# Six persistent places instead of four rotating ones for the split halves of the experts' weights, and two raw buffers fewer

## The chip, the core and the metric

One core of a Trainium2 chip runs the whole program. The metric is device time in microseconds (us), from start to end of one execution; the number given for a kernel is the median of several. Five engines of the core matter: PE (matrix multiplication), ACT (scalar engine), DVE (vector engine), POOL and SP. Here SP issues nearly all transfers.

## What is computed

The reference is a small network on 256 tokens of width 1024: a first block of four mixers with a feed-forward part, then a second block with a retention mixer, a dense feed-forward part, a Fourier mixer, and last a mixture of eight experts. All of it is float32. The experts are the part that the change is about:

```
def swiglu(t, w_gate, w_up, w_down):
    return (jax.nn.silu(t @ w_gate) * (t @ w_up)) @ w_down

def moe_swiglu(h, w_router, w_gate, w_up, w_down):
    ...
    top_val, top_idx = lax.top_k(logits, TOP_K)
    top_w = jax.nn.softmax(top_val, axis=-1)
    gates = jnp.sum(jax.nn.one_hot(top_idx, N_EXPERTS, dtype=jnp.float32) * top_w[..., None], axis=1)
    ...
    for e in range(N_EXPERTS):
        out = out + gates[:, e:e + 1] * swiglu(t, w_gate[e], w_up[e], w_down[e])
```

## The kernel before

All weights lie in memory as 475 units of 1 MB, a tile of 128 partitions by 2048 float32 each, in the order in which they are used. SP loads one unit after another into raw tiles. To multiply in float32 precision on PE, each weight is split into two parts that PE takes at full rate: ACT copies a half unit (128 by 1024) into `wh`, the rounded high part (line 128), and DVE subtracts it from the raw half into `wl`, the low part (line 129). So each of the 950 halves costs one ACT and one DVE instruction, and PE works on both parts. `split()` (line 117 on) writes these two instructions for the next half and appends the pair to the list `wq`; `half()` calls `split()` once and takes the oldest pair from the list, and with `ahead=False` it only takes. How far the splits run ahead of the matmuls in the written program is thus the length of `wq`. The tiles of `wh` and of `wl` rotate through a pool `wp` of four places each: the split of half n can't write before PE has read half n-4.

An expert runs 84 halves in seven strips. A strip s consists of
- a gate strip: four halves, six matmuls each (per half two blocks of `wh` with the high part of the tokens `ex`, `wh` with their low part, `wl` with their high part: lines 1142 to 1144). Between its second and third half stands `turn(s-1)`, eight small matmuls that transpose the previous strip's `h` (line 1194);
- `sg`, the Silu of the gate result on ACT (line 1177), which needs the last matmul of the gate strip;
- an up strip: four halves in two pairs;
- `h` on DVE (line 1184), the product of `sg` and the up result, which needs the last matmul of the up strip;
- `hx`, the split of the transposed previous `h` (ACT line 1200, DVE line 1201);
- `down(s-1)`: four halves in two pairs.

Pairs of halves in up and down stand in a branch that PE alone decides at run time (lines 1146 to 1153): an expert with at most 64 tokens takes the packed form, in which one matmul with line 1139 stands for the two of lines 1142 and 1143, so that PE has four matmuls per half instead of six. In the profiled execution experts 0, 2, 3 and 4 are packed, 1, 5, 6 and 7 are not. ACT and DVE do the same work in both.

Within an expert I count halves locally: strip s (from 1) has gate halves 8+12(s-1) to 11+12(s-1), then four of up, then four of down(s-1). Strip 3 thus has the gate halves 32 to 35, the up halves 36 to 39 and the down halves 40 to 43, and strip 4's gate halves begin at 44.

The order of PE and SP is the one in which the code is written. The order of ACT and DVE is set when the program is built, by a scheduler that places each instruction by a model of when its inputs are there; the engine then keeps that order. `turn`, `hx`, `sg` and `h` have a priority in it (`tc.high_priority`).

The raw tiles come from pools: `rawp` of 6 units, `raw2p` of 4, `raw3p` of 2, `raw4p` of 2 (opened just ahead of the experts), and the former tile of the tokens, `xT`, of 1: 15 in the experts. A raw tile is loaded anew as soon as both its halves are split.

Of the kernel before, what the change touches and what calls it, by code (L numbers as in the profile page):

```python
# [10 lines left out]
F32R = mybir.dt.float32r  # L11
# [5 lines left out]
P = 128  # L17
# [46 lines left out]
def kernel(  # L64
# [9 lines left out]
):  # L74
    nc = tc.nc
    NU = ws_d.shape[0]
    WB = 4
    HP = 300
    HQ = 512
    HU = UN // 2  # L80

    NRAW, R2N, R3N, R4N = 6, 4, 2, 2
    const = ctx.enter_context(tc.tile_pool(name="const", bufs=1))
    rawp = ctx.enter_context(tc.tile_pool(name="rawp", bufs=NRAW))
    wp = ctx.enter_context(tc.tile_pool(name="wp", bufs=WB))
    psp = ctx.enter_context(tc.tile_pool(name="psp", bufs=2, space=bass.MemoryType.PSUM))
    ctx.enter_context(tc.manual_schedule(engines={mybir.EngineType.PE, mybir.EngineType.SP}))

# [2 lines left out]
    wq = []  # L91
# [18 lines left out]
    def more_room(name, n):  # L110
        pool = ctx.enter_context(tc.tile_pool(name=name, bufs=n))
        for _ in range(n):
            fetch(pool)

    half_ = [0, 0]

    def split(scales=None, between=None):


        if not raw or (half_[1] == H_F2 and scales is None):  # L120
            return
        half_[1] += 1
        r = raw[0][0][:, half_[0] * HU:(half_[0] + 1) * HU]
        wh = wp.tile([P, HU], F32R, tag="wh", name="wh")
        wl = wp.tile([P, HU], F32R, tag="wl", name="wl")
        if scales is None:
            for o in (slice(0, HQ), slice(HQ, HU)) if half_[1] == 1 else (slice(0, HU),):
                nc.scalar.activation(out=wh[:, o], in_=r[:, o], func=AF.Copy)  # L128
                nc.vector.tensor_tensor(out=wl[:, o], in0=r[:, o], in1=wh[:, o].bitcast(F32), op=ALU.subtract)  # L129
                if between is not None and o.start == 0:  # L130
                    between()
        else:
            for t in range(2):
                o = slice(t * 512, t * 512 + 512)
                nc.scalar.activation(out=wh[:, o], in_=r[:, o], func=AF.Copy, scale=scales[:, t:t + 1])
                nc.vector.scalar_tensor_tensor(out=wl[:, o], in0=r[:, o], scalar=scales[:, t:t + 1],
                                               in1=wh[:, o].bitcast(F32), op0=ALU.mult, op1=ALU.subtract)
        wq.append((wh, wl))
        if half_[0]:
            fetch(raw.pop(0)[1])  # L140
        half_[0] ^= 1
# [8 lines left out]
    def advance(item):  # L150
        try:
            item[0] = next(item[1]) or 1
        except StopIteration:
            side.remove(item)
# [16 lines left out]
    def half(ahead=True):  # L171

        for item in list(side):
            item[0] -= 1
            if item[0] <= 0:
                advance(item)
        if ahead:
            split()
        return wq.pop(0)

    def bank(tag="mm", shape=(P, 2, S)):
        return psp.tile(list(shape), F32, tag=tag, name=tag, bufs={"mm": 4, "sd": 2, "dn": 2}[tag])
# [3 lines left out]
    def mm3T(ps, u, b, xh, xl, start, stop):  # L186
        wh, wl = u
        c = slice(b * P, (b + 1) * P)
        mm(ps, wh[:, c], xh, start=start, stop=False)  # L189
        mm(ps, wh[:, c], xl, start=False, stop=False)  # L190
        mm(ps, wl[:, c], xh, start=False, stop=stop)  # L191
# [10 lines left out]
    def unit_late(xh, xl, late=2):  # L202

        ps = [bank("mm", (P, S)) for _ in range(2)]
        us = []
        for cb in range(2):
            us.append(half())
            for k in range(KD - late):
                mm3T(ps[cb], us[cb], k, xh[:, k], xl[:, k], k == 0, False)
        for cb in range(2):  # L210
            for k in range(KD - late, KD):
                mm3T(ps[cb], us[cb], k, xh[:, k], xl[:, k], False, k == KD - 1)
        return ps

    def stripX(xh, xl, mid=None):
# [51 lines left out]
    def col(c, n=1):  # L267
        return cols[:, c:c + n]
# [94 lines left out]
    for c in range(2, KD, 2):  # L363
        resplit(c, 2, col(C_N1, 8))
    for _ in range(WB - 2):
        split()
# [692 lines left out]


    pt.close()
    if R4N:
        more_room("raw4p", R4N)
    xT_flat = xT.rearrange("p a b -> p (a b)")
    fetch(xT_flat)
    fn = xT_flat[:, 0:D]
    with ExitStack() as pe:
# [48 lines left out]
        def experts(ex, rs, half_fn, hooks=None, n_of=None):  # L1116
# [6 lines left out]
            n = [0]  # L1123
# [3 lines left out]
            def nexth(**kw):  # L1127
                if hooks and n[0] in hooks:
                    hooks[n[0]]()
                n[0] += 1  # L1130
                return half_fn(**kw)
# [76 lines left out]
            def down(s, mid=None):  # L1208
                def blocks(b0):
                    pair(lambda w, packed: hi_lo(ht[s], [down_item(s, b0 + i, w[i], hf) for i in range(2) for hf in range(2)],  # L1210
                                                 packed))

                blocks(0)
                if mid is not None:
                    mid()
                if s < 6:
                    blocks(2)
                else:

                    w = [nexth() for _ in range(2)]  # L1220
                    for hf in range(2):
                        either(lambda packed: hi_lo(ht[s], [down_item(s, b, w[b - 2], hf) for b in (2, 3)], packed))
                        with tc.high_priority(HP):
                            result(hf)

            res = []

            def result(hf):
                y = G2.tile([P, 2, 512], F32R, tag="hx", name="y")
                yh, yl = y[:, 0], y[:, 1]  # L1230
                nc.scalar.activation(out=yh, in_=pd[hf], func=AF.Copy)
                nc.vector.tensor_tensor(out=yl, in0=pd[hf], in1=yh.bitcast(F32), op=ALU.subtract)
                res.append((yh, yl))
# [30 lines left out]
        for i in (0, 2, 1, 3):  # L1264
            nxt[3][i]()
        finish_rms()
        last = None
        for e in range(E):
            ex, sot, rs, _ = nxt
# [34 lines left out]
        with tc.tile_pool(name="O", bufs=1) as O:  # L1304
            ecur = O.tile([P, E], F32, name="ecur")
            emask = O.tile([P, E], F32, name="emask")
            epos = O.tile([P, 2], F32, name="epos")
            egts = O.tile([P, 2], F32, name="egts")
            etmp = O.tile([P, 2, E], F32, name="etmp")
            with tc.If(n_over[0] + n_over[1] > 0):  # L1310

                nc.vector.tensor_copy(out=ecur, in_=io8)
                with tc.For_i(0, E, 1) as ev:
                    nc.vector.tensor_scalar(out=emask, in0=ecur, scalar1=-8.0, scalar2=None, op0=ALU.is_equal)
                    for src, dst in ((pos, epos), (gts, egts)):
                        nc.vector.tensor_tensor(out=etmp, in0=src, in1=emask.unsqueeze(1).to_broadcast([P, 2, E]), op=ALU.mult)
                        nc.vector.tensor_reduce(out=dst, in_=etmp, axis=AX.X, op=ALU.add)
                    nc.vector.tensor_scalar(out=epos, in0=epos, scalar1=float(-P), scalar2=None, op0=ALU.add)
                    cnt_ = [0]
                    cur_ = []  # L1320

                    def ohalf(ahead=True):
                        i, h = divmod(cnt_[0], 2)
                        if h == 0:
                            t = rawp.tile([P, UN], F32, tag="raw", name="oraw")
                            nc.sync.dma_start(t, ws_d[bass.ds(ev * UE + (NU - E * UE + i), 1)].rearrange("a p n -> p (a n)"))
                            cur_[:] = [t]
                        r = cur_[0][:, h * HU:(h + 1) * HU]
                        wh = wp.tile([P, HU], F32R, tag="wh", name="owh")
                        wl = wp.tile([P, HU], F32R, tag="wl", name="owl")  # L1330
                        nc.scalar.activation(out=wh, in_=r, func=AF.Copy)
                        nc.vector.tensor_tensor(out=wl, in0=r, in1=wh.bitcast(F32), op=ALU.subtract)
                        cnt_[0] += 1
                        return wh, wl

                    oex, osot, ors, steps = gather(lambda t: epos[:, t:t + 1], lambda t: epos[:, t:t + 1])
                    for f in steps:
                        f()
                    combine(experts(oex, ors, ohalf), osot, lambda t: egts[:, t:t + 1])
                    nc.vector.tensor_scalar(out=ecur, in0=ecur, scalar1=-1.0, scalar2=None, op0=ALU.add)  # L1340
                for hf in range(2):
                    out_sumsq(hf)
                out_rms()
# [172 lines left out]
```

## Time and profile before

| what | value |
|---|---|
| time, median of 3 runs | 1873.32 us (1871.12 to 1874.76) |
| time of the profiled execution | 1872.74 us |
| its span | 1871.0 us |
| PE busy | 1817.4 us, 97% of the span |
| DVE busy | 1482.0 us, 79% |
| ACT busy | 1210.6 us, 65% |
| POOL busy | 158.2 us, 8% |
| split of a half on DVE, line 129 | 906 instructions, 1227 ns each |
| split of a half on ACT, line 128 | 906 instructions, 1053 ns each |

The experts run from about 900 us to the end. The span is what the trace covers; the 1.7 us up to the time of the execution lie around it. In rows of the trace an instruction shows its start, its duration and, in brackets, the idle time of its engine ahead of it with what ended that. Consecutive instructions of an engine overlap a little, so that the step from start to start can be shorter than a duration.

### The profile page before, as it was taken

Reading aid. Unit: us, or ns where it says so; the run is one execution under the profiler, and the core shown is the slowest. Engines: PE = TensorE matmul, PEld = TensorE weight load, DVE = VectorE, ACT = ScalarE, POOL = GpSimd, SP = SyncE. Lnnn points to the kernel's source line nnn. Section 1 sums busy time; section 2 is a strip of 40 time slices with the busy share of each in tenths; the row PEclk is TensorE's granted clock in tenths of the full one; section 3 lists DMA queues with packets and bytes.
Section 4 is the critical chain, followed back from the end, with each engine's and each line's share of the span. In section 5 each row is a group of like instructions: output and inputs, shape, how many; then the busy total and the mean of one; then the engine's idle time right before and its main releaser. Section 6 shows DMA issues by size and latency. Waiting matters only on the chain. (4 is left out here: it accounts for less than half of the span.)

```text
span 1871.0 us, 28740 instructions
## 1 busy us (share of the span) xinstructions
PE 1817.4 (97%) x10890; PEld 1574.5 (84%) x10890; DVE 1482.0 (79%) x1855; ACT 1210.6 (65%) x1484; POOL 158.2 (8%) x154
## 2 busy tenths in 40 slices
PE   8999999999999999999999999999999999999997
PEld 7999999999888999998777887777777788888885
DVE  5666676657677666656899989999999998988987
ACT  5765454455344444446787777888878777777775
POOL 2302122211111122110000000000000000000000
PEclk9999999999999999999999999999999999999999
DMA  8344544555444564544799998999999999999970
GB/s 313 140 154 168 193 178 183 181 181 197 158 150 159 189 248 184 187 170 180 295 419 377 353 367 326 411 386 377 415 354 413 381 353 364 332 356 354 343 290 36
DMA packets 71156, 505.77 MB, mean 270 GB/s; under 512 B 7888, under 2 KB 8016, under 8 KB 10320
## 3 DMA queue, kind: packets, MB, share of 16 engines
q1 hardware_dynamic: 70992, 503.53, 70.7%
q8 instruction: 110, 1.80, 0.4%
q14 instruction: 54, 0.44, 0.1%
HBM read 502.45 MB, written 1.05 MB: 269 GB/s over the span
## 5 line engine op out<-in xcount | busy, mean ns | idle before, releaser
L129 DVE TENSOR_TENSOR wl<-raw,wh 128x1024 fp32r<-128x1024 f32 (+1 forms) x906 | 1078.5, 1227 | 235.3 <-ACT wh L128 226.2
L128 ACT ACTIVATE wh<-raw 128x1024 fp32r<-128x1024 f32 (+1 forms) x906 | 922.0, 1053 | 428.9 <-PE mm L190 188.7
L189 PE MATMUL mm<-xh,wh 128*128 128x256 f32 x1248 | 357.5, 286 | 6.7 <-ACT xh L342 6.7
L1144 PE MATMUL mm<-wl,ex 128*128 128x512 f32 x896 | 356.0, 397 | 3.7 <-DVE wl L129 3.7
L190 PE MATMUL mm<-xl,wh 128*128 128x256 f32 x1248 | 355.2, 285 | 1.0 <-DVE xl L343 0.7
L191 PE MATMUL mm<-xh,wl 128*128 128x256 f32 x1248 | 354.9, 284 | 0.8 <-DVE wl L129 0.8
L1142 PE MATMUL mm<-wh,ex 128*128 128x512 f32 x672 | 270.4, 402 | 0.0
L1143 PE MATMUL mm<-wh,ex 128*128 128x512 f32 x672 | 266.1, 396 | 0.2 <-DVE ex L1103 0.2
L189 PEld LDWEIGHTS mm<-xh,wh 128*128 128x128 f32 x1248 | 237.9, 191 | 8.2 <-ACT xh L342 6.7
L190 PEld LDWEIGHTS mm<-xl,wh 128*128 128x128 f32 x1248 | 237.9, 191 | 2.4 <-DVE xl L343 2.3
L191 PEld LDWEIGHTS mm<-xh,wl 128*128 128x128 f32 x1248 | 237.7, 190 | 1.1 <-DVE wl L129 1.0
L1144 PEld LDWEIGHTS mm<-wl,ex 128*128 128x128 f32 x896 | 168.6, 188 | 54.2 <-DVE wl L129 13.7
L1144 PE MATMUL dn<-wl,hx 128*128 128x512 f32 x448 | 183.6, 410 | 12.1 <-DVE wl L129 11.9
L1143 PEld LDWEIGHTS mm<-wh,ex 128*128 128x128 f32 x672 | 126.7, 189 | 28.2 <-DVE ex L1103 0.5
L1142 PEld LDWEIGHTS mm<-wh,ex 128*128 128x128 f32 x672 | 126.6, 188 | 26.0 <-ACT wh L128 0.3
L1144 PEld LDWEIGHTS dn<-wl,hx 128*128 128x128 f32 x448 | 84.2, 188 | 55.8 <-DVE wl L129 40.1
L190 PE MATMUL mm<-hl,wh 128*128 128x256 f32 x352 | 99.8, 283 | 0.0
L191 PE MATMUL mm<-hh,wl 128*128 128x256 f32 x352 | 99.8, 283 | 0.0
L189 PE MATMUL mm<-hh,wh 128*128 128x256 f32 x352 | 99.8, 283 | 0.0
L1139 PE MATMUL dn<-wh,hx 128*128 128x512 f32 x224 | 89.2, 398 | 0.0
L1142 PE MATMUL dn<-wh,hx 128*128 128x512 f32 x224 | 88.9, 397 | 0.0
L1139 PE MATMUL mm<-wh,ex 128*128 128x512 f32 x224 | 88.7, 396 | 0.0
(400 smaller groups left out, 2500.7 us busy)
## 6 DMA issues: line engine op xcount, KB each, us to landing
raw<-in_ws_dram SPq DMA_DIRECT2D x451, 1024.0 KB, 6.3
xT<-in_ws_dram SPq DMA_DIRECT2D x22, 1024.0 KB, 7.0
raw<-in_ws_dram SPq DMA_DIRECT2D x3, 512.0 KB, 6.3
xT<-in_xT_dram SPq DMA_DIRECT2D x4, 256.0 KB, 5.4
xT<-in_xT_dram SPq DMA_DIRECT2D x1, 1024.0 KB, 8.3
out_dram<-acc SPq DMA_DIRECT2D x4, 256.0 KB, 2.1
cstA<-in_cst_dram SPq DMA_DIRECT2D x1, 576.0 KB, 9.1
raw<-in_ws_dram SPq DMA_DIRECT2D x2, 256.0 KB, 4.5
```

The costliest lines, as they stand in the source:

```text
L128: nc.scalar.activation(out=wh[:, o], in_=r[:, o], func=AF.Copy)
L129: nc.vector.tensor_tensor(out=wl[:, o], in0=r[:, o], in1=wh[:, o].bitcast(F32), op=ALU.subtract)
L189: mm(ps, wh[:, c], xh, start=start, stop=False)
L190: mm(ps, wh[:, c], xl, start=False, stop=False)
L191: mm(ps, wl[:, c], xh, start=False, stop=stop)
L1139: mm(out_, e, wh, start=first, stop=False)
L1142: mm(out_, e, wh, start=first, stop=False)
L1143: mm(out_, xk[:, P:2 * P], wh, start=False, stop=False)
L1144: mm(out_, e, wl, start=False, stop=last)
```

## The change

In the code before, `wp.tile(...)` is asked for each half. Now two tiles of four places (`ringh`, `ringl`) are made once, and two tiles of two places (`extrah`, `extral`) just ahead of the experts, in the memory that `raw4p` had. The function `place(i)` says which place the i-th split writes: one of four until the extra tiles exist, then one of six in turn. The written program splits further ahead: two more halves before the first expert (the `while`), and `half(ahead=not cb)` and `nexth(ahead=False)` with a `split()` behind the pair where `half()` had split for each half of a pair. So five halves stand in `wq` where three stood.

```
-    WB = 4
+    WB, WX = 4, 2
...
-    NRAW, R2N, R3N, R4N = 6, 4, 2, 2
+    NRAW, R2N, R3N = 6, 4, 2
...
-    wp = ctx.enter_context(tc.tile_pool(name="wp", bufs=WB))
+    wp = ctx.enter_context(tc.tile_pool(name="wp", bufs=1))
+
+    ring = [wp.tile([P, WB, HU], F32R, name=f"ring{n}") for n in "hl"]
+    extra = []
+
+    def place(i):
+        if extra and i >= extra[0]:
+            j = (i - extra[0]) % (WB + WX)
+            if j < WX:
+                return [x[:, j] for x in extra[1]]
+            i = extra[0] + j - WX
+        return [x[:, i % WB] for x in ring]
...
+        wh, wl = place(half_[1])
         half_[1] += 1
         r = raw[0][0][:, half_[0] * HU:(half_[0] + 1) * HU]
-        wh = wp.tile([P, HU], F32R, tag="wh", name="wh")
-        wl = wp.tile([P, HU], F32R, tag="wl", name="wl")
...
-            us.append(half())
+            us.append(half(ahead=not cb))
...
+        split()
         return ps
...
-    if R4N:
-        more_room("raw4p", R4N)
+    wp3 = ctx.enter_context(tc.tile_pool(name="wp3", bufs=1))
+    extra[:] = [half_[1], [wp3.tile([P, WX, HU], F32R, name=f"extra{n}") for n in "hl"]]
...
-                    w = [nexth() for _ in range(2)]
+                    w = [nexth(), nexth(ahead=False)]
...
+                    if half_fn is half:
+                        split()
...
+        while len(wq) < WB + WX - 1:
+            split()
```

The raw buffers of the experts are 13 instead of 15. No engine gets an instruction more or less. What moves is the order on ACT and DVE. In the kernel after, line 128 is line 139, 129 is 140, 1177 is 1189, 1184 is 1196, 1200 is 1212 and 1201 is 1213.

First, ACT in strip 3 of expert 2 (packed). Before: the row of four is halves 33 to 36, the next row is 37, the two ahead of `sg` are 38 and 39, and half 40 stands behind it.

```order
684 L128 ACTIVATE wh<-raw 128x1024 x4
685 L1150 UNCONDITIONAL_BRANCH
686 L128 ACTIVATE wh<-raw 128x1024
687 L1200 ACTIVATE hx<-sd 128x4x128
688 L128 ACTIVATE wh<-raw 128x1024 x2
689 L1177 ACTIVATE sg<-mm,rsl 128x512
690 L1150 UNCONDITIONAL_BRANCH
691 L128 ACTIVATE wh<-raw 128x1024
```

After: rows 742 and 743 are halves 33 to 35, row 745 is 36 and 37, and row 748, behind `sg`, is 38.

```order
742 L139 ACTIVATE extrah<-raw 128x1024
743 L139 ACTIVATE ringh<-raw 128x1024 x2
744 L1162 UNCONDITIONAL_BRANCH
745 L139 ACTIVATE ringh<-raw 128x1024 x2
746 L1212 ACTIVATE hx<-sd 128x4x128
747 L1189 ACTIVATE sg<-mm,rsl 128x512
748 L139 ACTIVATE extrah<-raw 128x1024
749 L1162 UNCONDITIONAL_BRANCH
750 L139 ACTIVATE extrah<-raw 128x1024
```

`sg` of strip 3 stood behind half 39 and stands behind half 37. It is so in strips 2 to 6 of experts 2 to 7 and in strips 4 to 6 of expert 1. In expert 0 and in the strips of expert 1 ahead of these, the row reads the other way: there, halves 38, 39, 40 and 41 (or those that answer to them) stand ahead of `sg`.

Second, DVE at the same place. Before: rows 1109 to 1117 are halves 36 to 42, row 1119 is 43, row 1120 is 44.

```order
1109 L129 TENSOR_TENSOR wl<-raw,wh 128x1024
1110 L1201 TENSOR_TENSOR hx<-sd,hx 128x4x128
1111 L129 TENSOR_TENSOR wl<-raw,wh 128x1024 x2
1112 L1150 UNCONDITIONAL_BRANCH
1113 L129 TENSOR_TENSOR wl<-raw,wh 128x1024 x2
1114 L1150 UNCONDITIONAL_BRANCH
1115 L129 TENSOR_TENSOR wl<-raw,wh 128x1024
1116 L1150 UNCONDITIONAL_BRANCH
1117 L129 TENSOR_TENSOR wl<-xT,wh 128x1024
1118 L1184 SCALAR_TENSOR_TENSOR h<-mm,rsl,sg 128x512
1119 L129 TENSOR_TENSOR wl<-xT,wh 128x1024
1120 L129 TENSOR_TENSOR wl<-raw,wh 128x1024
```

After: row 1117 is halves 36 and 37, rows 1120 to 1124 are 38 to 43, and row 1127 is 44 and 45.

```order
1117 L140 TENSOR_TENSOR ringl<-raw,ringh 128x1024 x2
1118 L1213 TENSOR_TENSOR hx<-sd,hx 128x4x128
1119 L1162 UNCONDITIONAL_BRANCH
1120 L140 TENSOR_TENSOR extral<-raw,extrah 128x1024 x2
1121 L1162 UNCONDITIONAL_BRANCH
1122 L140 TENSOR_TENSOR ringl<-xT,ringh 128x1024 x2
1123 L1162 UNCONDITIONAL_BRANCH
1124 L140 TENSOR_TENSOR ringl<-raw,ringh 128x1024 x2
1125 L1196 SCALAR_TENSOR_TENSOR h<-mm,rsl,sg 128x512
1126 L1162 UNCONDITIONAL_BRANCH
1127 L140 TENSOR_TENSOR extral<-raw,extrah 128x1024 x2
```

`h` of strip 3 moves from behind half 42 to behind half 43, and `hx` from behind half 36 to behind half 37. In strip 0 of an expert, `h` moves from behind half 10 to behind half 11.

Third, ACT in strip 3 of expert 5 of the kernel before: here, too, only halves 36 (row 989) and 37 (row 991) stand ahead of `sg`, and half 38 is the first behind it.

```order
989 L128 ACTIVATE wh<-raw 128x1024
990 L1200 ACTIVATE hx<-sd 128x4x128
991 L128 ACTIVATE wh<-raw 128x1024
992 L1177 ACTIVATE sg<-mm,rsl 128x512
993 L128 ACTIVATE wh<-raw 128x1024
994 L1150 UNCONDITIONAL_BRANCH
995 L128 ACTIVATE wh<-raw 128x1024 x2
```

It is so in experts 5 to 7 before, which are not packed in the profiled execution; in the changed kernel that expert's order is that of expert 2 above.

## Rows read from the trace of the kernel before

**Rows 1.** The page: engine, busy us, share of the span, instructions.

```profile
PE 1817.4 (97%) x10890; PEld 1574.5 (84%) x10890; DVE 1482.0 (79%) x1855; ACT 1210.6 (65%) x1484; POOL 158.2 (8%) x154
```

**Rows 2.** Windows: us, busy of PE, PEld, DVE, ACT, POOL, PE clock, DMA share, GB/s.

```profile
1200.00:1300.00 100.00, 95.17 (x423) 72.24 (x422) 97.87 (x100) 81.93 (x92) 0.00 (x0) 1.00 0.97 384
...
1600.00:1700.00 100.00, 99.96 (x446) 80.63 (x445) 88.02 (x87) 75.83 (x83) 0.00 (x0) 1.00 0.92 349
```

**Rows 3.** Timeline of DVE, a packed strip: start, us, instruction, [idle before <-releaser].

```profile
1211.00 0.74 DVE L1184 SCALAR_TENSOR_TENSOR h<-mm,rsl,sg 128x512 f32<-128x512 f32 x1
1211.66 6.89 DVE L129 TENSOR_TENSOR wl<-raw,wh 128x1024 fp32r<-128x1024 f32 x6
1218.57 0.69 DVE L1201 TENSOR_TENSOR hx<-sd,hx 128x512 fp32r<-128x512 f32 x1
1219.18 7.13 DVE L129 TENSOR_TENSOR wl<-raw,wh 128x1024 fp32r<-128x1024 f32 x6
1226.22 0.75 DVE L1184 SCALAR_TENSOR_TENSOR h<-mm,rsl,sg 128x512 f32<-128x512 f32 x1
```

**Rows 4.** Timeline of ACT, the same strip.

```profile
1218.79 1.06 ACT L128 ACTIVATE wh<-raw 128x1024 fp32r<-128x1024 f32 x1 [0.26 <-PE mm L1143]
1220.19 1.06 ACT L128 ACTIVATE wh<-raw 128x1024 fp32r<-128x1024 f32 x1 [0.34 <-PE mm L1143]
1221.16 0.67 ACT L1177 ACTIVATE sg<-mm,rsl 128x512 f32<-128x512 f32 x1
1221.73 6.74 ACT L128 ACTIVATE wh<-raw 128x1024 fp32r<-128x1024 f32 x7
```

**Rows 5.** Timeline of PE, the same strip.

```profile
1212.93 0.50 PE L1144 MATMUL dn<-wl,hx 128*128 128x512 f32 x1 [0.59 <-DVE wl L129]
...
1214.20 0.39 PE L1144 MATMUL mm<-wl,ex 128*128 128x512 f32 x1
...
1219.99 0.39 PE L1144 MATMUL mm<-wl,ex 128*128 128x512 f32 x1
1220.22 0.40 PE L1139 MATMUL mm<-wh,ex 128*128 128x512 f32 x1
```

**Rows 6.** Timeline of PE, a strip of expert 5, not packed.

```profile
1568.42 0.40 PE L1144 MATMUL mm<-wl,ex 128*128 128x512 f32 x1
...
1571.92 0.39 PE L1144 MATMUL mm<-wl,ex 128*128 128x512 f32 x1
```

**Rows 7.** Timeline of ACT, the strip of rows 6.

```profile
1566.54 1.05 ACT L128 ACTIVATE wh<-xT 128x1024 fp32r<-128x1024 f32 x1
1568.85 0.69 ACT L1177 ACTIVATE sg<-mm,rsl 128x512 f32<-128x512 f32 x1 [1.26 <-PE mm L1144]
1569.44 3.89 ACT L128 ACTIVATE wh<-raw 128x1024 fp32r<-128x1024 f32 x4
```

**Rows 8.** Timeline of DVE, the strip of rows 6.

```profile
1567.95 1.22 DVE L129 TENSOR_TENSOR wl<-xT,wh 128x1024 fp32r<-128x1024 f32 x1
1570.52 3.50 DVE L129 TENSOR_TENSOR wl<-raw,wh 128x1024 fp32r<-128x1024 f32 x3 [1.35 <-ACT wh L128]
```

**Rows 9.** Timeline of PE, first strips of expert 0.

```profile
912.27 0.50 PE L1144 MATMUL mm<-wl,ex 128*128 128x512 f32 x1 [0.53 <-DVE wl L129]
...
915.60 1.13 PE L1194 MATMUL sd<-cst,h 128*128 128x128 f32 x8 [0.73 <-DVE h L1184]
```

**Rows 10.** Timeline of DVE, first strip of expert 0 and boundary to expert 4.

```profile
910.99 2.36 DVE L129 TENSOR_TENSOR wl<-raw,wh 128x1024 fp32r<-128x1024 f32 x2 [1.72 <-ACT wh L128]
...
1362.78 1.22 DVE L129 TENSOR_TENSOR wl<-raw,wh 128x1024 fp32r<-128x1024 f32 x1 [1.13 <-ACT wh L128]
```

**Rows 11.** Timeline of PE, the Fourier mixer's projection.

```profile
849.19 0.36 PE L912 MATMUL mm<-wh,fh 128*128 128x256 f32 x1 [1.14 <-issue]
```

**Rows 12.** DMA issues in 1200 to 1500 us: count, size, median us to landing.

```profile
raw<-in_ws_dram SPq DMA_DIRECT2D x103, 1024.0 KB, 7.5
```

More of the change, by code (lines that the diff above doesn't have):

```diff
@@ L1328, in ohalf @@
                         r = cur_[0][:, h * HU:(h + 1) * HU]
-                        wh = wp.tile([P, HU], F32R, tag="wh", name="owh")
-                        wl = wp.tile([P, HU], F32R, tag="wl", name="owl")
+                        wh, wl = (x[:, cnt_[0] % WB] for x in ring)
                         nc.scalar.activation(out=wh, in_=r, func=AF.Copy)
```

## The prediction

> **What bounds the kernel now.** I read the share of busy time first: PE 97%, DVE 79% [rows 1]. As an average this says that PE is the limit everywhere. The table by windows corrects it. In the experts that are not packed PE is busy 99.96% of a window and DVE 88%; in the packed experts it is DVE that is at 97.87% and PE at 95.17% [rows 2]. So the experts have two limits: PE in 1, 5, 6 and 7, DVE in 0, 2, 3 and 4, and a change of the split order has to be judged in each.
>
> The timeline of DVE gives a packed strip's length: `h` at 1211.00 and again at 1226.22, 15.22 us apart, and every later strip repeats it [rows 3]. What DVE does in it: six splits back to back show 6.89 us busy; less the last one's duration of 1.22 that is 5.67 for five steps, 1.134 a step. Twelve steps are 13.61, `h` holds DVE for 0.66 (1211.00 to 1211.66) and `hx` for 0.61 (1218.57 to 1219.18): 14.88. DVE has 0.34 us to spare per strip, and no more can be won there while the work stays the same.
>
> PE waits in such a strip for single `wl`: one split starts at 1211.66 and its first matmul at 1212.93, after 0.59 us of idle [rows 3, 5]. So a `wl` that is waited for costs 1.27 us from its start to PE.
>
> **What the change removes, adds and moves.** No instruction is added or taken away. Three things differ: places, raw buffers, and the order on ACT and DVE.
>
> The places come first, because they are what lets splits run ahead. Before, ACT waited in a packed strip twice for a place, 0.26 and 0.34 us, each ended by a matmul [rows 4]; these waits did not hold DVE, which had a row of six behind it. With six places they go. Nothing is won by that alone, since DVE's spare 0.34 per strip is all there is.
>
> The order is what decides. Before, in the packed experts half 39 is the last ahead of `sg`: the whole up strip is split when ACT turns to wait for the gate strip's last matmul. After, only halves 36 and 37 are, and half 38 is behind `sg`. A written look-ahead of five halves becomes one of two at this point, as the scheduler put `sg` earlier by its priority. ACT keeps its order, so what queues behind `sg` is the `wh` of half 38 and with it DVE's whole row of six.
>
> What this costs is to be seen in the trace of before, because experts 5 to 7 have that order already. There the last gate matmul starts at 1568.42; ACT, idle for 1.26 us, starts `sg` at 1568.85, 0.43 later; the next `wh` at 1569.44, 0.59 later; the `wl` at 1570.52, 1.08 later, after DVE had been idle for 1.35 us [rows 6 to 8]. From the last gate matmul to the `wl` are 2.10 us, and to PE 1.27 more: 3.37. In an unpacked strip PE takes 3.50 us from there to the half in question (1568.42 to 1571.92, [rows 6]): a margin of 0.13, and no stall. In a packed strip PE has only the last gate matmul and eight packed ones in front of it, at one step of 0.23 each (1219.99, 1220.22; [rows 5]), plus the `wh` matmul of that half: ten steps, 2.33. So PE runs dry for 3.37 - 2.33 = 1.04 us in each packed strip, and DVE, which has no time to spare, stands still for longer than it can make up.
>
> Now the cycle of a packed strip, from the `wl` of half 38 at 0:
> - six splits (38 to 43), 6 x 1.134: 6.80;
> - `h`, which now stands behind half 43: 0.66, to 7.46;
> - half 44, the first of the next gate, reaches PE 1.27 later: 8.73, the third matmul of the strip;
> - from the third matmul to the last gate matmul 5.79 (1214.20 to 1219.99, with the turn, [rows 5]): 14.52. DVE's further splits come every 1.134, and PE takes six steps of 0.23, 1.40, for a gate half, so they are not late;
> - `sg` 0.43, `wh` 0.59, `wl` 1.08: 16.62, where half 50 begins as half 38 did.
>
> 16.62 against 15.22 is **+1.40 us** per strip. Of the 16.62 DVE works 14.88, so its idle rises from 0.34 to 1.74. Bounds: the least is that nothing new is waited for and DVE wins its 0.34 (-0.34); the most is that the 2.10 behind `sg` come on top of a DVE that had all else to do, 14.88 + 2.10 = 16.98 (+1.76). I take +1.40 since all its terms have rows.
>
> [...]
>
> The sum by experts:
> - experts 2, 3, 4: from strip 2's `sg` to strip 6's there are four such cycles, 4 x 1.40 = 5.6. At strip 0 `h` stands one split later than before, at most 1.13, and the turn waits for it; at least 0; I take half, 0.6. 6.2 each, **+18.6**.
> - expert 0 keeps the good order: five strips lose their idle of 0.34, -1.7. Two splits more lie ready at its start, -2 x 1.134 = -2.3; they remove the 0.53 and 0.73 that PE stalls in its first strips and most of DVE's gap of 1.72 [rows 9, 10]. They stand now among the small steps of the router, which the first matmuls wait for, so something between 0 and 2.3 comes back; I take 0.6, as ACT held DVE up there anyway. **-3.4**.
> - expert 1 is bound by PE and keeps the good order up to strip 3: 0.
> - experts 5 to 7: the order in the strips is the one they had, so the margin of 0.13 stays; only the later `h` of strip 0 counts, again between 0 and 1.13; nearer to 0 as PE has work: 0.5 each, **+1.5**.
> - the Fourier mixer's projection: one split earlier and the next ones later; it can take away at most the stall of 1.14 [rows 11], at least nothing: **-0.8**.
> - two raw buffers fewer: a unit lands in 7.5 us [rows 12]. Thirteen units cover 12 x 2 halves of 1.27 us (15.22 by 12), 30 us, from the moment that a tile is free. That leaves 23 where 28 were: 0.
>
> Together +18.6 - 3.4 + 1.5 - 0.8 = +15.9. The sum is made against the profiled execution, 1872.74 us (span 1871.0); its median of three is 1873.32, so the two can be taken as one. 1872.7 + 15.9 = **1888.6**, 0.85% slower.
>
> **The rivals.**
> *Faster: more places, no bubble.* If ACT's order didn't bind (the half behind `sg` reaching PE within the 2.33 us of a packed strip), look-ahead would carry each packed expert to DVE's own floor: 7 x 0.34 and the 1.13 that DVE idles at a boundary [rows 10], 3.5 each, four of them 14.0; with two splits ahead (-1.7 net) and Fourier, 1856; half of it, 1864. For it: DVE and PE wait for each other in small pieces, as is usual with too few places. Against: 3.37 is more than 2.33 by rows on both sides. Chance 0.12, time about 1861. [...]
> *No change:* the wait behind `sg` replaces the old waits almost one for one, say +0.4 a strip (PE's stall of 1.04 less the 0.59 that goes). 12 x 0.4 + 1.8 + 1.5 - 3.4 - 0.8 = +3.9, and with the boundary gains of 1.13 in three experts +0.5: 1873. Against it: DVE's idle adds up in full, as it has no slack. Chance 0.08.
> *Slower still:* the unpacked experts' margin of 0.13 does not hold, since raw data or places shift by some tenths. Some 18 strips at 0.3: +5.4, 1894. It decides once the `wl` behind `sg` is over 0.13 later than in rows 8. Chance 0.17.
> *Raw buffers:* transfers come late in packed strips. It would need 23 us more than the 7.5 shown. Chance 0.03, time above 1900.
>
> **How the numbers follow.** The forecast has 0.60, with 1883 to 1893 as its own range (the half-splits and +1.40 moved by 0.3 a strip). Slower by over 0.2%, which is about what a measurement of this kernel can tell from no change, are the forecast, the worse one and the raw buffers: 0.80. Within it: 0.08. Faster: 0.12. The range leaves out the faster case and a little at the top: 1872 to 1900.
>
> **What would show it.** Right: in experts 2 to 4 the `h` are 16.6 apart, DVE shows one idle of some 1.7 us per strip ended by ACT's `wh`, directly behind `sg`; ACT waits there on the last gate matmul; PE stalls about 1 us ahead of the up strip's second pair and again at half 44; DVE's share in the windows falls to some 90%. Expert 0 is a few us shorter, and in experts 5 to 7 DVE and PE look as in rows 6 to 8. Wrong: strips of 14.9 to 15.2 in experts 2 to 4 (the order doesn't bind), PE stalls in experts 5 to 7 (the margin), or raw tiles that end DVE's or ACT's idle time (DMA).

## The result and the profile after

The changed kernel takes 1899.74 us (median of 4 runs, 1897.26 to 1901.95) against 1873.5 us of the kernel before (median of 4): a ratio of 1.0141, 95% interval 1.0124 to 1.0159. It is slower by 26.2 us where 15.9 were forecast; the time lies 0.26 us below the upper end of the range, 1900, and two of the four runs lie above it. The profiled execution has a span of 1898.4 us, 27.4 above that of before.

The page of the changed kernel, busy time of the engines (compare [rows 1]): the same work, in a longer span.

```profile
PE 1827.2 (96%) x10890; PEld 1576.7 (83%) x10890; DVE 1474.8 (78%) x1855; ACT 1198.2 (63%) x1484; POOL 158.6 (8%) x154
```

Its windows, with the columns of [rows 2]:

```profile
1200.00:1300.00 100.00, 92.68 (x405) 68.67 (x404) 92.30 (x95) 75.03 (x86) 0.00 (x0) 1.00 0.96 361
...
1600.00:1700.00 100.00, 99.27 (x446) 80.04 (x445) 88.38 (x89) 73.06 (x83) 0.00 (x0) 1.00 0.92 347
```

In the packed stretch DVE falls from 97.87% to 92.30% and PE from 95.17% to 92.68%: both wait more, so neither limits alone. The unpacked stretch hardly moves.

The timeline of DVE in a packed strip of expert 2, to be laid beside [rows 3]:

```profile
1203.00 0.75 DVE L1196 SCALAR_TENSOR_TENSOR h<-mm,rsl,sg 128x512 f32<-128x512 f32 x1
1203.66 2.35 DVE L140 TENSOR_TENSOR extral<-raw,extrah 128x1024 fp32r<-128x1024 f32 x2
1205.93 4.63 DVE L140 TENSOR_TENSOR ringl<-raw,ringh 128x1024 fp32r<-128x1024 f32 x4
1210.47 0.69 DVE L1213 TENSOR_TENSOR hx<-sd,hx 128x512 fp32r<-128x512 f32 x1
1212.92 2.36 DVE L140 TENSOR_TENSOR extral<-raw,extrah 128x1024 fp32r<-128x1024 f32 x2 [1.75 <-ACT extrah L139]
1215.19 4.63 DVE L140 TENSOR_TENSOR ringl<-raw,ringh 128x1024 fp32r<-128x1024 f32 x4
1219.74 0.75 DVE L1196 SCALAR_TENSOR_TENSOR h<-mm,rsl,sg 128x512 f32<-128x512 f32 x1
```

From `h` to `h` are 16.74 us instead of 15.22, with one idle of 1.75, ended by ACT. ACT at that place, compare [rows 4]:

```profile
1211.25 0.69 ACT L1189 ACTIVATE sg<-mm,rsl 128x512 f32<-128x512 f32 x1 [2.21 <-PE mm L1156]
1211.83 2.00 ACT L139 ACTIVATE extrah<-raw 128x1024 fp32r<-128x1024 f32 x2
```

ACT has been idle for 2.21 us, waiting for the gate strip's last matmul, and the `wh` for which DVE is idle stands directly behind `sg`. PE in the same strip, compare [rows 5]:

```profile
1204.93 0.50 PE L1156 MATMUL mm<-extral,ex 128*128 128x512 f32 x1 [0.37 <-DVE extral L140]
1205.27 0.40 PE L1154 MATMUL mm<-extrah,ex 128*128 128x512 f32 x1
...
1210.82 0.39 PE L1156 MATMUL mm<-ringl,ex 128*128 128x512 f32 x1
...
1214.20 0.50 PE L1156 MATMUL mm<-extral,ex 128*128 128x512 f32 x1 [0.77 <-DVE extral L140]
```

PE stalls where the forecast had it: 0.37 us at the gate strip's first `wl` and 0.77 us at the first `wl` of the up strip's second pair.

Where the 27.4 us of the two spans lie, reckoned from the starts of `h` in strip 0 of each expert (up to there from PE's matmuls, at about 800 and 866 us of the kernel before):

| stretch | before, us | after, us | difference | forecast |
|---|---|---|---|---|
| start to the Fourier mixer | | | +1.9 | 0 |
| Fourier mixer's projection | | | +1.3 | -0.8 |
| from there to `h` of strip 0 in expert 1 | | | -0.7 | -3.4 |
| expert 1 (to the same `h` of expert 2) | 126.00 | 126.99 | +1.0 | 0 |
| experts 2, 3, 4 | 113.72, 113.72, 113.94 | 120.76, 120.73, 121.82 | +21.9 | +18.6 |
| experts 5, 6 and 7 | 125.90, 125.90, 123.42 | 126.47, 126.50, 124.22 | +2.0 | +1.5 |

The first line is no effect of the change: in the runs below PE's matmuls at 44 us stand between 1.5 us earlier and 1.8 us later than in the kernel before, also in `before_early` and `before_13raw`, which have the order of the kernel before up to there. Since `h` itself moved against PE's matmuls, some tenths of the lines by expert belong to their neighbours.

### The profile page after: what moved, and what is told of

The parts are those of the page before. It is cut to its first block, busy times and chain, and to the rows that moved or that the text cites. A ratio compares the mean times of both kernels' runs of the same rounds, so it can differ in the third digit from the quotient of the medians.

```text
span 1898.4 us, 28758 instructions
## 1 busy us (share of the span) xinstructions
PE 1827.2 (96%) x10890; PEld 1576.7 (83%) x10890; DVE 1474.8 (78%) x1855; ACT 1198.2 (63%) x1484; POOL 158.6 (8%) x154
## 5 line engine op out<-in xcount | busy, mean ns | idle before, releaser
L140 DVE TENSOR_TENSOR ringl<-raw,ringh 128x1024 fp32r<-128x1024 f32 (+1 forms) x694 | 828.7, 1228 | 191.9 <-ACT ringh L139 186.6
L139 ACT ACTIVATE ringh<-raw 128x1024 fp32r<-128x1024 f32 (+1 forms) x694 | 703.4, 1050 | 309.0 <-PE mm L201 192.1
L200 PE MATMUL mm<-xh,ringh 128*128 128x256 f32 x1248 | 357.4, 286 | 6.4 <-ACT xh L354 6.4
L202 PE MATMUL mm<-xh,ringl 128*128 128x256 f32 x1248 | 354.7, 284 | 1.5 <-DVE ringl L140 1.5
L201 PE MATMUL mm<-xl,ringh 128*128 128x256 f32 x1248 | 355.1, 285 | 1.0 <-DVE xl L355 0.7
L140 DVE TENSOR_TENSOR extral<-raw,extrah 128x1024 fp32r<-128x1024 f32 x206 | 244.4, 1221 | 66.3 <-ACT extrah L139 66.3
L200 PEld LDWEIGHTS mm<-xh,ringh 128*128 128x128 f32 x1248 | 238.0, 191 | 7.8 <-ACT xh L354 6.4
L201 PEld LDWEIGHTS mm<-xl,ringh 128*128 128x128 f32 x1248 | 237.8, 191 | 2.3 <-DVE xl L355 2.1
L1154 PE MATMUL mm<-ringh,ex 128*128 128x512 f32 x352 | 144.4, 410 | 0.0
L1155 PE MATMUL mm<-ringh,ex 128*128 128x512 f32 x352 | 139.8, 397 | 0.2 <-DVE ex L1115 0.2
L1154 PE MATMUL mm<-extrah,ex 128*128 128x512 f32 x320 | 125.5, 392 | 0.0
L1155 PE MATMUL mm<-extrah,ex 128*128 128x512 f32 x320 | 125.4, 392 | 0.0
```

Source lines behind the costliest of these rows:

```text
L1154: mm(out_, e, wh, start=first, stop=False)
L1155: mm(out_, xk[:, P:2 * P], wh, start=False, stop=False)
```

## Experiments

Two theories stood against each other. One: the order on ACT costs the time, since what queues behind `sg` waits with it. The other: the resources cost it, six places or two raw buffers fewer.

**The order alone, in the changed kernel (`order`).** One edge for the scheduler is added, with a helper `behind(a, b)` that makes it place `a` behind `b`: `sg` goes behind the last split written ahead of it, which is half 40 in strip 3.

```
-                nc.scalar.activation(out=sg[s], in_=ps, func=AF.Silu, scale=rs)
+                sgi = nc.scalar.activation(out=sg[s], in_=ps, func=AF.Silu, scale=rs); behind(sgi, last_a[0]) if half_fn is half else None
```

> The changed kernel with one thing altered: on ACT sg must stand behind the last split written ahead of it, so that halves 38, 39 and 40 are split before ACT turns to wait for the gate strip. Places, raw buffers and look-ahead as in the changed kernel. Theory (the order on ACT costs the time): strips of experts 2 to 4 fall from 16.73 to DVE's own 14.9, these experts from 120.8-121.8 to about 112.2 us, some 26 us together, and the time from 1899.7 to 1874 (1870 to 1878). Rival (the two raw buffers or the six places themselves cost it): strips stay over 16, the time 1895 or more.

It took 1871.2 us (1867.17 to 1875.45; 10 runs), 0.9993 of the kernel before, 0.9982 to 1.0004. The timeline of DVE in a strip of expert 2:

```profile
1196.39 0.77 DVE L1196 SCALAR_TENSOR_TENSOR h<-mm,rsl,sg 128x512 f32<-128x512 f32 x1
1197.06 2.38 DVE L140 TENSOR_TENSOR extral<-raw,extrah 128x1024 fp32r<-128x1024 f32 x2
1199.32 4.65 DVE L140 TENSOR_TENSOR ringl<-raw,ringh 128x1024 fp32r<-128x1024 f32 x4
1203.86 0.72 DVE L1213 TENSOR_TENSOR hx<-sd,hx 128x512 fp32r<-128x512 f32 x1
1204.46 2.38 DVE L140 TENSOR_TENSOR extral<-raw,extrah 128x1024 fp32r<-128x1024 f32 x2
1206.73 4.66 DVE L140 TENSOR_TENSOR ringl<-raw,ringh 128x1024 fp32r<-128x1024 f32 x4
1211.27 0.78 DVE L1196 SCALAR_TENSOR_TENSOR h<-mm,rsl,sg 128x512 f32<-128x512 f32 x1
```

ACT in that strip has no wait at `sg`:

```profile
1204.27 1.05 ACT L139 ACTIVATE ringh<-raw 128x1024 fp32r<-128x1024 f32 x1
1205.21 0.68 ACT L1189 ACTIVATE sg<-mm,rsl 128x512 f32<-128x512 f32 x1
```

No idle of DVE is left, the strips are 14.88 us long, and experts 2 and 3 take 111.0 us, expert 4 112.8. So some 28 us of the changed kernel's time go with this order (the three experts alone give 28.5), and the places and raw buffers stay as changed. Six places with this order bring what [rows 3] had as spare: 15.22 falls to 14.88, and no further. The whole is the same as the kernel before within what the runs can tell.

**The order alone, in the kernel before (`before_early`).** The `wh` of the next half to be written goes behind `sg`; four places, 15 raw buffers and the look-ahead stay.

```
+                behind(last_a[0], due.pop()) if due else None
...
-                nc.scalar.activation(out=sg[s], in_=ps, func=AF.Silu, scale=rs)
+                sgi = nc.scalar.activation(out=sg[s], in_=ps, func=AF.Silu, scale=rs); due.append(sgi) if half_fn is half else None
```

> The kernel before with one thing altered: on ACT sg stands ahead of the wh of half 38, in all experts. Four places, 15 raw buffers and the look-ahead as before. Theory (the order costs the time): packed strips grow from 15.22 to 16.7, five in each of experts 0, 2, 3 and 4, 7 us each, so 1873.5 + 28 = 1901 (1896 to 1907); experts 1 and 5 to 7 do not move. Rival (it takes six places or 13 raw buffers to lose): below 1880.

1910.21 us (1908.82 to 1912.21), a ratio of 1.0198, 1.0179 to 1.0216. DVE in a packed strip:

```profile
1204.71 4.63 DVE L129 TENSOR_TENSOR wl<-raw,wh 128x1024 fp32r<-128x1024 f32 x4 [1.70 <-ACT wh L128]
...
1210.39 0.75 DVE L1185 SCALAR_TENSOR_TENSOR h<-mm,rsl,sg 128x512 f32<-128x512 f32 x1
...
1227.17 0.75 DVE L1185 SCALAR_TENSOR_TENSOR h<-mm,rsl,sg 128x512 f32<-128x512 f32 x1
```

and ACT ahead of that idle:

```profile
1203.05 0.69 ACT L1178 ACTIVATE sg<-mm,rsl 128x512 f32<-128x512 f32 x1 [1.89 <-PE mm L1145]
1203.63 3.89 ACT L128 ACTIVATE wh<-raw 128x1024 fp32r<-128x1024 f32 x4
```

The strips are 16.77 us long, with the idle of the changed kernel, in experts 0, 2, 3 and 4; experts 1 and 5 to 7 keep their length within 0.1 us. It is more than expected by 9 us. Some 6 of them are strip 0, which was not counted: there `sg` stands early too, and it grows from 10.98 to 12.22 us in experts 2 to 4 and from 10.66 to 13.12 in expert 0. The other 3 are the five strips, 1.55 us each where 1.4 were reckoned. The loss needs neither the places nor the missing buffers. That ACT keeps its order is to be seen in the rows: it idles 1.89 us at `sg` here and starts the `wh` behind it only then, 0.58 us after `sg` (1203.05 to 1203.63), and DVE idles 1.70 us for it; with that `wh` ahead of `sg`, in the kernel before, DVE has no such idle [rows 3].

**One half more ahead of `sg` (`look3`).** The look-ahead is written so that `sg` stands directly behind half 38, and the `wh` of half 39 behind `sg`.

```
+                behind(last_a[0], due.pop()) if due else None
...
+                sgi = nc.scalar.activation(out=sg[s], in_=ps, func=AF.Silu, scale=rs); (behind(sgi, last_a[0]), due.append(sgi)) if half_fn is half else None
...
-        while len(wq) < WB + WX - 1:
+        while len(wq) < 3:
```

> The changed kernel with a look-ahead written one half longer than two: sg stands directly behind half 38 and the wh of half 39 behind sg, in experts 2 to 4 in strips 2 to 6. The cycle as reckoned has one split less between sg's wait and the next gate strip: 5 x 1.134 + 0.66 + 1.27 + 5.89 + 2.10 = 15.59 us against 16.73 with half 37. Theory: strips of 15.6 in experts 2 to 4, some 17 us less than the changed kernel in all, 1882 (1878 to 1886). Rival (what is lost is a fixed wait at sg, not work that queues behind it): strips stay at 16.7, or fall at once to 14.9.

1883.75 us in one run. DVE of expert 2:

```profile
1197.71 1.22 DVE L140 TENSOR_TENSOR extral<-raw,extrah 128x1024 fp32r<-128x1024 f32 x1 [0.53 <-ACT extrah L139]
...
1213.31 1.22 DVE L140 TENSOR_TENSOR extral<-raw,extrah 128x1024 fp32r<-128x1024 f32 x1 [0.53 <-ACT extrah L139]
```

The strip is 15.60 us long, and the idle 0.53. With six places, a strip with half 37 as the last ahead of `sg` takes 16.73, with 38 15.60, with 40 14.88, which is DVE's own work; no run with six places has 39 there. So one half more ahead of `sg`, 38, is worth one DVE step, 1.13 us, and two more only the 0.72 that are left until DVE has no idle. That bears out the cycle that the forecast was made from. The whole time is a weaker witness: expert 0, where the order moved as well, takes 117.9 us instead of 112.2, and other stretches make up for it.

**Six places with the old look-ahead (`places2`).** The two extra splits ahead of the first expert and the edit in `down(6)` are taken back.

```
-                    w = [nexth(), nexth(ahead=False)]
+                    w = [nexth() for _ in range(2)]
...
-        while len(wq) < WB + WX - 1:
-            split()
```

> The changed kernel with the experts' look-ahead written as in the kernel before (three halves in the list, no extra splits ahead of the first expert); six places and 13 raw buffers as changed. On ACT sg stands behind half 37 in experts 2 to 7 here too. Theory (the order counts, not the number of halves written ahead): strips of 16.7 in experts 2 to 4, about 1898. Rival (the longer written look-ahead is what costs): strips of 15.2 or less, about 1875.

1897.81 us in one run; strips of 16.70 to 16.73 in experts 2 to 4. It costs the same whether three or five halves are written ahead: where the scheduler puts `sg` decides. An earlier form of it, `places` (1886.29 us), also took back the edit in the Fourier mixer's projection, which by the code sends a split into a place still in use; in it other experts were packed, so its time can't be compared. Its packed strips with `sg` early were 16.7 us long as well.

**Two raw buffers fewer in the kernel before (`before_13raw`).**

```
-    NRAW, R2N, R3N, R4N = 6, 4, 2, 2
+    NRAW, R2N, R3N, R4N = 6, 4, 2, 0
```

> The kernel before with 13 raw buffers instead of 15 and nothing else. Theory (transfers have 20 us and more of cover): 1873.5, within 2 us. Rival (fewer raw buffers cost a part of what was lost): 1880 or more, with splits that wait for transfers.

1878.27 us (1875.76 to 1881.44; 10 runs), a ratio of 1.0025, 1.0015 to 1.0034: slower by 4.7 us by the ratio, 5.6 by the medians, which the theory had not expected. But it is not as the rival has it: no split of the experts waits for a transfer, and from 1200 to 1500 us a unit lands in 7.4 us where it took 7.5 [rows 12]. Experts 0 to 3 are as before; expert 4 takes 118.76 us instead of 113.94, and there stands the known picture, first ACT, then DVE:

```profile
1434.74 0.69 ACT L1177 ACTIVATE sg<-mm,rsl 128x512 f32<-128x512 f32 x1 [1.26 <-PE mm L1144]
```

```profile
1436.41 4.63 DVE L129 TENSOR_TENSOR wl<-raw,wh 128x1024 fp32r<-128x1024 f32 x4 [1.67 <-ACT wh L128]
```

In the kernel before, the scheduler goes over to the early `sg` in expert 5; with 13 raw buffers it does so in expert 4: half 38 is the last ahead of `sg` in strip 3 (15.63 us), and in strips 4 to 6 it is the second of the up strip (16.77 us each). The missing buffers cost 4.8 us of this execution by way of the order.

**Eleven raw buffers, the order held (`order_11raw`).** `order` with `R3N = 0`.

```
-    NRAW, R2N, R3N = 6, 4, 2
+    NRAW, R2N, R3N = 6, 4, 0
```

> The run order with two raw buffers fewer still, 11 instead of 13; the order on ACT in the experts is pinned as there. Theory (transfers have some 20 us of cover, and the 5.6 us of the run before_13raw came from an order that tipped in expert 4): within 2 us of order's 1871.2, strips of 14.9 in experts 2 to 4. Rival (fewer raw buffers cost time by themselves): 1876 or more, with splits that wait for transfers.

1868.11 us (1866.62 to 1873.02; 10 runs), 0.9971 of the kernel before (0.9961 to 0.9982), strips of 14.88. The DMA issues in 1200 to 1500 us and the waits of DVE from 900 us on:

```profile
raw<-in_ws_dram SPq DMA_DIRECT2D x102, 1024.0 KB, 8.1
```

```profile
DVE extral L140 <- DMA raw<-in_ws_dram: 0.3, 1, 0.3
```

One wait of 0.3 us for a transfer in all the experts. The cover by raw buffers is ample, as forecast, with four fewer than before. The median is 3.1 us below that of `order` where 2 were allowed for; between the two profiled executions experts 2 to 7 differ by 0.1 us at most, and what differs lies ahead of the Fourier mixer (1.4 us) and between it and `h` of strip 0 in expert 1 (1.2 us), where PE's clock fell in `order` alone (last section). So these runs show no gain by fewer buffers.

**`h` of strip 0 earlier (`order_h`, `best`).** What stays of the loss in expert 0 is shown by DVE of the changed kernel at its first strip:

```profile
914.08 2.36 DVE L140 TENSOR_TENSOR ringl<-raw,ringh 128x1024 fp32r<-128x1024 f32 x2 [1.72 <-ACT ringh L139]
916.40 1.23 DVE L140 TENSOR_TENSOR extral<-raw,extrah 128x1024 fp32r<-128x1024 f32 x1
917.54 1.22 DVE L140 TENSOR_TENSOR ringl<-raw,ringh 128x1024 fp32r<-128x1024 f32 x1
918.68 0.75 DVE L1196 SCALAR_TENSOR_TENSOR h<-mm,rsl,sg 128x512 f32<-128x512 f32 x1
```

and by PE, to be compared with [rows 9]:

```profile
919.57 2.05 PE L1206 MATMUL sd<-cst,h 128*128 128x128 f32 x8 [2.71 <-DVE h L1196]
```

`h` stands behind halves 10 to 13, DVE's gap of 1.72 is still there, and `turn(0)` waits 2.71 us for `h` where it waited 0.73. `order_h` is `order` with the split behind the up strip's second pair written behind `h`, and held there:

```
-            def pair(f):
+            def pair(f, more=True):
...
-                if half_fn is half:
+                if half_fn is half and more:
...
-                    pair(lambda w, packed: [hi_lo(ex, strip_items(ps, h + i, w[i]), packed) for i in range(2)])
+                    pair(lambda w, packed: [hi_lo(ex, strip_items(ps, h + i, w[i]), packed) for i in range(2)], h == 0)
...
-                nc.vector.scalar_tensor_tensor(out=hq[s], in0=ps, scalar=rs, in1=sg[s], op0=ALU.mult, op1=ALU.mult)
+                hi = nc.vector.scalar_tensor_tensor(out=hq[s], in0=ps, scalar=rs, in1=sg[s], op0=ALU.mult, op1=ALU.mult)
+                if half_fn is half:
+                    split()
+                    behind(last_v[0], hi)
```

> As the run before, and besides h stands one split earlier on DVE where the written order sets it (a split that was written ahead of h is written behind it); this moves it in expert 0 alone to any effect. Theory (the start of expert 0 lost about 4 us since PE's turn waited 2.71 us for an h behind two needless splits, and the clock fell behind it): 2 to 4 us below the run before, 1871. Rival (the start lost its time elsewhere): the same as the run before.

1865.88 us (1863.59 to 1866.07; 5 runs), 0.9962 of the kernel before, 0.9948 to 0.9976: faster than it and than `order`. In its expert 0 `turn(0)` waits 1.58 us instead of 2.71, with PE's clock at 1.00 behind it (914 to 920 us). Not all of the 5.3 us below `order` are `h`'s doing: of the 6.6 between the two profiled executions 2.6 lie ahead of the experts, 1.6 of them in the Fourier mixer, where the clock fell in `order` alone (0.50 in 854 to 856 us). In experts 4 and 5 `turn(0)` still waits, 1.83 and 1.70 us:

```profile
1371.25 1.76 PE L1209 MATMUL sd<-cst,h 128*128 128x128 f32 x8 [1.83 <-DVE h L1196]
```

```profile
1484.04 0.66 PE L1211 MATMUL sd<-cst,h 128*128 128x128 f32 x4 [1.70 <-DVE h L1196]
```

`best` moves one split more behind `h` in strip 0, which brings `h` there behind half 10 in experts 2 to 7, as before the change (against `order_h`):

```
-            def pair(f, more=True):
+            def pair(f, more=True, ahead=True):
...
-                w = [nexth(), nexth(ahead=False)]
+                w = [nexth(ahead=ahead), nexth(ahead=False)]
...
-                    pair(lambda w, packed: [hi_lo(ex, strip_items(ps, h + i, w[i]), packed) for i in range(2)], h == 0)
+                    pair(lambda w, packed: [hi_lo(ex, strip_items(ps, h + i, w[i]), packed) for i in range(2)], h == 0, h == 0 or s > 0)
...
+                    if s == 0:
+                        split()
```

> The run order_h with one edit more: in strip 0 of an expert two splits that were written ahead of h are written behind it, so that h stands behind half 10 as in the kernel before, not behind half 11. Theory (the stalls of 1.70 us at turn(0) of experts 5 to 7 and of 1.83 at that of expert 4 are the wait for this h): 1.6 us less in each of experts 5 to 7 and some 2 in expert 4, about 1859.5 against 1865.9. Rival (turn(0) waits for something else, or DVE loses as much by the earlier wait): 1864 or more.

1863.55 us (1862.33 to 1865.33; 5 runs), 0.9954 of the kernel before, 0.9940 to 0.9967. The row of expert 5 that answers to the last one above:

```profile
1486.27 0.65 PE L1213 MATMUL sd<-cst,h 128*128 128x128 f32 x4 [0.58 <-DVE h L1196]
```

At `turn(0)` PE waits 1.1 us less in each of experts 5, 6 and 7, not 1.6, since `h` moved by one DVE step; expert 4 stays at 112.8, as in `order`, whose strips are at DVE's own 14.88 us; from that I estimate that PE waits for `wl` later what it no longer waits for `h`. In expert 0 `turn(0)` waits 2.71 us again, as DVE idles 1.10 us for a `wh` among the splits ahead of `h`, and from PE's first matmul with `wl` to the same in expert 1 it takes 110.4 us instead of 109.2. So the rows give 3 x 1.1 less 1.2, 2.2 us. The gain over `order_h` by the medians is 2.3 us where 6.4 were expected; the time lies just below the rival's 1864, and the intervals of the two runs overlap: that `best` is the faster one is likely by its rows, not settled by its times. That either beats both kernels is settled.

## Why the forecast was right, and where it fell short

The direction and the mechanism were right; that the time fell inside the range is luck. The range held the median by 0.26 us, and the interval of the ratio reaches up to 1903. In the profiled executions the sum was 11.5 us short (27.4 against 15.9): 3.3 in experts 2 to 4, 2.7 around expert 0, 2.1 in the Fourier mixer, 1.0 in expert 1, 0.5 in experts 5 to 7, and 1.9 at the start by chance.

**The bound by experts** held: the packed experts 2 to 4 moved by 7 to 8 us each, the unpacked ones by 0.6 to 1.0.

**The mechanism** held in each part: the idle behind `sg` (16.73 less 14.88 of work is 1.85, where 1.74 were forecast; 1.75 in one row), its releaser, the two places where PE stalls (0.77 and 0.37 us; some 1 us at the first was forecast), and expert 0's strips at DVE's floor (14.88 measured; forecast 15.22 less 0.34). The margin of 0.13 us in the unpacked strips held too: their later strips are 17.14 us long, 17.20 before. The rival that ACT's order doesn't bind fell with `before_early`, that of late transfers with `order_11raw`; that fewer buffers can tip the scheduler's order was in no rival.

**The cycle** was 16.73 where I had 16.62. The missing 0.11 stands in the rows of PE: the first matmul behind a stall takes 0.34 (1204.93 to 1205.27) until the next one starts, not 0.23, so that from the gate strip's third matmul to its last are 5.89, not the 5.79 of [rows 5]. The 0.23 is also all that the traces show of a full rate of PE on the two parts of a weight: in the kernel before, matmuls of unsplit float32 of the same 128x512 (line 786) start 0.43 us apart, both at a granted clock of 1.00.

**The count** of cycles was wrong. I took four from `sg` of strip 2 to that of strip 6; between the `h` of strip 1 and of strip 6 lie five, all of 16.73. That is 5 x 1.51 = 7.6 instead of 5.6 for an expert, and it is the largest error of the sum: 2 us in each of three experts. Strip 0 and the boundary hid a part of it: +0.7 in strip 0 (11.64 against 10.98), where I had 0.6 for the later `h`, and -1.2 in the boundary (25.47 against 26.63), which I had left out. In sum +7.0 against 6.2; expert 4 lost 0.8 more, behind a fall of the clock (last section). Whether the later `h` is what strip 0 cost is not shown: `order_h` and `best` differ in it, and experts 2 and 3 take 111.0 us in both.

**Expert 0** missed by 2.7 us. My sum has no term for its `h`, and where the change is described I had it one split later in every expert; the order has it behind half 13, three later (in expert 1 behind 12, two later). Instead of the wait of 0.73 us at `turn(0)` going away there is one of 2.71, and DVE's gap of 1.72, most of which was to go, stayed. A part is the clock, which fell behind that wait. `order_11raw` has the same order and the same wait in expert 0, but kept the full clock behind it, as the duration of the eight matmuls shows (2.05 us in the changed kernel):

```profile
916.50 1.13 PE L1206 MATMUL sd<-cst,h 128*128 128x128 f32 x8 [2.71 <-DVE h L1196]
```

Its strip 0 takes 10.66 us, that of `order` 12.05 and that of the changed kernel 12.22. From the Fourier mixer to the `h` of strip 0 in expert 1, `order` is 0.8 us shorter than the kernel before, `order_11raw` 2.0, and `order_h`, with that `h` one split earlier, 4.9 us: the gain forecast was there to be had.

**The Fourier mixer** came out at +1.3 for -0.8. Its first stalls did not go, they grew: 1.14 and 0.27 us before [rows 11], 1.74 and 0.79 after. It is not the edit in the projection itself that lengthened them, as `places`, which takes it back, has the same two; what did is open. But most of the loss is the clock, and that can't be put down to the change alone. From the first to the last matmul of the projection PE takes 9.26 us in the kernel before and 11.30 in the changed one. `before_13raw`, whose ACT and DVE have the order of the kernel before there and the same stalls, takes 10.78, and `order_h`, with the stalls of the changed kernel, 9.74. The windows of the two, first `before_13raw`:

```profile
852.00:854.00 2.00, 2.00 (x11) 2.00 (x11) 1.80 (x4) 1.22 (x2) 0.00 (x0) 0.50 0.82 344
```

```profile
852.00:854.00 2.00, 2.00 (x20) 1.83 (x18) 0.72 (x3) 0.93 (x4) 0.00 (x0) 1.00 0.79 233
```

So the fall costs 1.5 us with either order, and the longer stalls 0.5, which shorter waits behind give back: the stretch of the table is 0.2 us shorter in `order_h` than in the kernel before and 1.7 longer in `before_13raw`. The clock fell there in one of the three profiled executions with the shorter stalls and in seven of the eight with the longer ones, which speaks for the longer stalls making it likelier but does not settle it. My bound at nothing for the worse side had no reason.

**Expert 1** lost 1.0 by the marks of the table where I had nothing, but the marks moved: from PE's first matmul with `wl` in it to the same in expert 2 it takes 127.11 us before and 127.14 after. Its `turn(0)` does wait 1.28 us for DVE where it waited 0.04. The trace names `acc` as what it waited for, which stands next to `h` there; no run tells the two apart.

## What to carry to other kernels

A look-ahead written in the source is worth what the order on the engine leaves of it: count the work that stands ahead of the instruction that waits, not the places. An item that slipped behind it here, half 38, cost 1.13 us in each strip, one step of DVE (15.60 us in `look3`, 16.73 in the changed kernel); halves 39 and 40 together cost 0.72, since the 14.88 of `order` is DVE's own work. After an edit that touches buffers alone, compare the order again: two raw buffers fewer moved an instruction, and that cost 4.8 us, while no split waited for a transfer. And look at the granted clock before a difference of 1 or 2 us in one stretch is put down to an edit.

## What was not expected of the hardware

PE's granted clock fell to 0.50 behind some stalls, and behind equal ones it did not. The windows of the changed kernel behind the wait of 2.71 us in expert 0 (columns as in [rows 2]):

```profile
916.00:918.00 2.00, 0.86 (x4) 0.38 (x2) 2.00 (x3) 2.00 (x3) 0.00 (x0) 1.00 0.57 180
918.00:920.00 2.00, 0.43 (x2) 0.46 (x3) 2.00 (x3) 1.21 (x2) 0.00 (x0) 0.87 0.89 352
920.00:922.00 2.00, 2.00 (x10) 1.90 (x10) 1.69 (x2) 0.34 (x1) 0.00 (x0) 0.50 0.42 139
922.00:924.00 2.00, 2.00 (x9) 1.59 (x8) 0.69 (x1) 0.79 (x2) 0.00 (x0) 0.77 0.86 348
```

It is 1.00 again from 924 us on; PE lost some 1.5 us more by it, an estimate from strip 0, which took 12.22 us here and 10.66 in `order_11raw`, where the clock stayed. It fell likewise behind the Fourier mixer's stalls (0.50 in 856 to 858 us, 1.00 there before) and behind a wait of 2.00 us at `turn(0)` of expert 4 (0.50 in 1401 to 1403 us), where strip 0 took 12.64 us instead of 11.65 in expert 3. Together that is some 4 us of the 27.4, an estimate from these three stretches. But behind the same wait of 2.00 us in experts 2 and 3 it stayed at 1.00, and so it did behind the 2.71 us of expert 0 in `order_11raw` (its eight matmuls in 1.13 us, those of the changed kernel in 2.05); and in the Fourier mixer it fell in `before_13raw` too, where nothing had moved. Which of equal stalls it falls behind these runs do not tell. Behind the stalls of 0.37 and 0.77 us in the packed strips it stayed at 1.00.
